# Four mLSTM projections as sixteen pairs of seven products each, made ahead of the attention, with the convolution summed in a PSUM bank

## The chip, the cores and the metric

One core of a Trainium2 chip. The metric is the device time of one execution of the whole program, in microseconds (us). The program works in fp32; matrix products run in the fp32r format, three of them for each product (below).

## The reference

A block on x (1024 positions, 1024 channels) with two branches and a gated sum. Cut to what matters:

```python
h = rmsnorm(x, norm_g)
proj = einsum('bsd,de->bse', h, w_in)      # a_q a_k a_v a_o a_z a_g b_q b_k b_v b_z g_a g_b, 1024 columns each, a_g 16
qk = silu(centred_depthwise_conv(concat([a_q, a_k]), ml_conv_w))    # width 5, along the sequence
mq, mk, mv = heads(qk[:1024]), heads(qk[1024:]) / 16, heads(a_v)    # 4 heads of 256
hm = rmsnorm(mlstm(forward) + mlstm(backward), ml_norm_g)           # gates from a_g
y_a = hm * sigmoid(a_o) * silu(a_z)
att = rmsnorm(diff_attention(rope(b_q), rope(b_k), b_v, lam), da_subln_g) * (1 - lambda_init)   # 8 heads
y_b = att * silu(b_z)
mix = sigmoid(g_a + gb0) * (y_a @ w_branch_a) + sigmoid(g_b + gb1) * (y_b @ w_branch_b)
return rmsnorm(x + mix @ w_out, final_g)
```

## The kernel before, in words

Every fp32 matrix is held as a high part (H, rounded to fp32r) and a low part (L, the rest), and a product of two is three fp32r products into one PSUM bank: wH x hH, wH x hL, wL x hH. A weight block of 128 columns (`load_w`) comes by DMA into `raw`; ScalarE copies it to `wH`, and GpSimd (POOL) or, in the mLSTM, VectorE subtracts to get `wL`. `proj` makes one block's product with half the sequence: 8 steps of k by three parts, 24 matmuls of 128x512 into one of the two banks `pj`. `v_units` makes v with 256 columns at a time, 192 matmuls of 128x256 a head.

The program is laid out by `build` as a list of units with costs and due times; `Weaver.weave` merges lists by when a unit is ready (table `LAG`) and by its share of its list. What comes out is each engine's order; nothing reorders it on the chip. The stages: x is loaded, normalised and transposed (TensorE, `transpose_x`), split into `hH`, `hL` (`split_h`); the attention's angles and rotary tables; eight attention heads; the mLSTM (pool `w2`), four heads, here numbered 0 to 3; the two branch products and the output.

`fill(n)` gives n units of the gates g_a and g_b, 48 matmuls each, which may stand anywhere; the table `FILL` says how many stand at each place.

In the mLSTM a head n goes through `ml_proj`: the projections of v, k and q, with the convolution on VectorE over the whole 1024 positions in SBUF (`cin` to `acc` or `hm`, L803), a split of the result into akH, akL, aqH, aqL (L808, L809), and a second list `oz`, the o and z projections, whose eight 24-matmul units are woven into the head's core. `ml_core` works in chunks of 256 positions, both directions. A state step transposes k (L130, into a bank T), weighs it into kwH and kwL (ScalarE L882, VectorE L883), multiplies it with v (L126) and adds it to the state C (L904, L906), which is split into CH and CL (L916, L917). Then come eight tiles of scores: SS = k x q, I = state x q (one bank each), weights W on VectorE (L947, L954), denominators (L961 to L970), W scaled and summed over directions (L974, L976), its transposes, their split WH and WL (L994, L995), PO = W x v, and hm, the sum of I and PO (L982, L1006). At the end of each head y_a is formed with the gates `gA`, made of `oz` (L824 to L831).

```python
            pr, oz = self.ml_proj(n, stm[n])
            core, tail, out = self.ml_core(n, stm[n])
            cut = len(pr) * 2 // 3
            w.weave(late, pr[:cut])
            w.add(*pr[cut:])
            w.weave(core, oz + fill(FILL[10 + n]))
            late = tail + out
```

## Time and profile before

| | |
|---|---|
| three runs | 1762.59 to 1762.73 us, median 1762.73 |
| the profiled execution | 1761.77 us, its span 1760.1 |
| TensorE clock granted, mean | 0.994 |
| TensorE busy | 1700.8 us |
| VectorE busy | 990.7 us |
| ScalarE busy | 709.7 us |
| GpSimd busy | 320.6 us |
| mean DMA rate | 90 GB/s |

The span is from the first to the last instruction of the profiled execution; 1.67 us of its time lie around it. Shares and busy times are means over stages with different limits, so the mLSTM, the opening and the attention are read by windows of their own.

### The profile page before, as it was taken

How to read it: one execution, taken by the hardware profiler on the slowest of the kernel's cores; microseconds unless marked ns; L12 is line 12 of the kernel's file. 1: busy time of each engine (PE TensorE's matmuls, PEld its weight loads, DVE VectorE, ACT ScalarE, POOL GpSimd, SP SyncE). 2: the span in 40 equal slices, each digit the busy share in tenths (PEclk: the TensorE clock that was granted, in tenths of full speed). 3: DMA queues.
4: the chain of work that ended last, by engine and by line, in shares of the span. 5: the costliest groups of instructions: out<-in, count | busy, mean ns of one | idle time of the engine just before them, and what ended most of it. 6: DMA issues, size and time to landing. Idle time of an engine off the chain costs nothing.

```text
span 1760.1 us, 23869 instructions
## 1 busy us (share of the span) xinstructions
PE 1700.8 (97%) x9311; PEld 1449.3 (82%) x9311; DVE 990.7 (56%) x1915; ACT 709.7 (40%) x1354; POOL 320.6 (18%) x300
## 2 busy tenths in 40 slices
PE   6999899999999999999999999999999999999998
PEld 5788788879878987887888888888888888888886
DVE  6326466666666665542577476656838743125533
ACT  5225455444445554441344344434434433122211
POOL 2323142331243233111000000100000002222000
PEclk9999999999999999999999999999999999999999
DMA  4445252345154515213210221121111117444222
GB/s 160 120 108 128 65 137 68 78 127 138 42 134 106 129 36 149 82 50 96 78 48 25 61 63 34 49 72 42 43 48 61 37 43 265 136 142 134 84 85 83
DMA packets 146787, 157.74 MB, mean 90 GB/s; under 512 B 7881, under 2 KB 106594, under 8 KB 146674
## 3 DMA queue, kind: packets, MB, share of 16 engines
q1 hardware_dynamic: 146498, 156.19, 31.5%
q8 instruction: 73, 1.20, 0.3%
q14 instruction: 40, 0.33, 0.1%
q10 hardware_dynamic: 176, 0.02, 0.0%
HBM read 118.31 MB, written 37.88 MB: 89 GB/s over the span
## 4 chain that ended last, share of the span: by engine, by line
PE 84%; DVE 4%; DMA 3%; POOL 3%; issue 3%; ACT 2%; SPq 0%; POOLq 0%; DVEq 0%; ACTq 0%
PE pj L242 50%; PE pj L264 9%; PE S L656 5%; PE PV L692 4%; PE pj L1149 4%; PE T L130 4%; PE T L126 2%; PE I L126 2%; PE SS L126 1%; PE PO L126 1%; DMA stk<-hl 1%; DMA rb<-rsd 1%; POOL m L599 1%; DMA qL<-stk 1%; ACT e L660 1%
## 5 line engine op out<-in xcount | busy, mean ns | idle before, releaser
L242 PE MATMUL pj<-hH,wH 128*128 128x512 f32 x1152 | 466.0, 404 | 7.6 <-ACT gt L568 4.6
L242 PE MATMUL pj<-hH,wL 128*128 128x512 f32 x1152 | 456.8, 397 | 0.6 <-POOL wL L185 0.6
L242 PE MATMUL pj<-hL,wH 128*128 128x512 f32 x1152 | 456.4, 396 | 0.0
L242 PEld LDWEIGHTS pj<-hH,wL 128*128 128x128 f32 x1152 | 217.3, 189 | 53.7 <-POOL wL L185 1.1
L242 PEld LDWEIGHTS pj<-hH,wH 128*128 128x128 f32 x1152 | 217.5, 189 | 52.9 <-ACT gt L568 5.0
L242 PEld LDWEIGHTS pj<-hL,wH 128*128 128x128 f32 x1152 | 217.5, 189 | 44.8
L660 ACT ACTIVATE e<-S,nm 128x1024 f32<-128x1024 f32 x128 | 143.0, 1117 | 186.6 <-DVE nm L658 186.4
L681 DVE TENSOR_TENSOR pL<-T,pH 128x512 fp32r<-128x512 f32 x128 | 87.9, 687 | 150.6 <-ACT pH L680 150.5
L658 DVE TENSOR_REDUCE nm<-S 128x1 f32<-128x1024 f32 x128 | 155.7, 1217 | 23.8 <-PE S L656 23.6
L200 POOL TENSOR_TENSOR wL<-raw,wH 128x1024 fp32r<-128x1024 f32 x45 | 109.1, 2425 | 308.6 <-ACT wH L195 301.5
L195 ACT CAST wH<-raw 128x1024 fp32r<-128x1024 f32 x88 | 92.3, 1049 | 172.6 <-PE pj L242 137.3
L264 PE MATMUL pj<-wH,hH 128*128 128x256 f32 x512 | 143.6, 281 | 0.0
L264 PE MATMUL pj<-wL,hH 128*128 128x256 f32 x512 | 143.2, 280 | 0.0
L264 PE MATMUL pj<-wH,hL 128*128 128x256 f32 x512 | 143.0, 279 | 0.0
L242 PE MATMUL pj<-sl_yb,wH 128*128 128x512 f32 x384 | 119.1, 390 | 0.3 <-DVE sl_yb L1065 0.2
L264 PEld LDWEIGHTS pj<-wH,hH 128*128 128x128 f32 x512 | 96.0, 187 | 1.1
L264 PEld LDWEIGHTS pj<-wH,hL 128*128 128x128 f32 x512 | 96.2, 188 | 0.8
L264 PEld LDWEIGHTS pj<-wL,hH 128*128 128x128 f32 x512 | 96.1, 188 | 0.0
L198 DVE TENSOR_TENSOR wL<-raw,wH 128x512 fp32r<-128x512 f32 x86 | 57.5, 691 | 64.9 <-ACT wH L195 64.4
L667 DVE SCALAR_TENSOR_TENSOR e<-e,r,e 128x1024 f32<-128x1024 f32 x64 | 92.7, 1448 | 1.2
L656 PE MATMUL S<-kst,qH 128*128 128x512 f32 x256 | 90.2, 432 | 2.7 <-DMA kst<-stk 2.7
L680 ACT CAST pH<-T 128x512 fp32r<-128x512 f32 x128 | 74.7, 583 | 32.5 <-PE T L130 29.5
(312 smaller groups left out, 3048.6 us busy)
## 6 DMA issues: line engine op xcount, KB each, us to landing
raw<-in_w_in_dram SPq DMA_DIRECT2D x88, 512.0 KB
stk<-hl SPq DMA_DIRECT2D x64, 256.0 KB
qH<-stk SPq DMA_DIRECT2D x32, 256.0 KB
qL<-stk SPq DMA_DIRECT2D x32, 256.0 KB
kst<-stk SPq DMA_DIRECT2D x16, 512.0 KB
x<-in_x_dram SPq DMA_DIRECT2D x8, 512.0 KB
tgb<-gt SPq DMA_DIRECT2D x16, 256.0 KB
rb<-rsd SPq DMA_DIRECT2D x16, 256.0 KB
```

The source lines that it names most:

```text
L126: self.t.matmul(out, lhsT=l, rhs=r, start=(i == 0), stop=(i == n - 1))
L130: self.t.transpose(out, in_, self.ident[0:k, 0:k])
L195: self.a.copy(wH, raw)
L200: self.p.tensor_tensor(out=wL, in0=raw, in1=wHf, op=ALU.subtract)
L242: self.t.matmul(ps, lhsT=l[:, k, :], rhs=r, start=(n == 0), stop=(n == 23))
L264: self.t.matmul(ps[:, i, :], lhsT=l, rhs=r[:, k, :], start=(kh == 0 and k == 0 and m == 0), stop=(kh == 1 and k == 3 and m == 2))
L656: self.t.matmul(ps[:, o], lhsT=x[:, j, c], rhs=st["k"][:, j, o], start=first, stop=not first)
L658: v.tensor_reduce(out=nm, in_=ps, axis=AX.X, op=ALU.max, negate=True)
L660: a.activation(out=e, in_=ps, func=AF.Exp, bias=nm[:, 0:1], accum_out=Z[:, j, t:t + 1])
L667: v.scalar_tensor_tensor(out=e0, in0=e, scalar=r[:, 0:1], in1=e0, op0=ALU.mult, op1=ALU.add)
L680: a.copy(pH[:, :, s], ps)
L681: v.tensor_tensor(out=pL[:, :, s], in0=ps, in1=pH[:, :, s].bitcast(F32), op=ALU.subtract)
```

## The change

The products of q, k, o and z leave the mLSTM. Two weight blocks of 128 columns, both halves of the sequence and both halves of the sum over channels make a product of 2x2 by 2x2 blocks, which is done with seven block products in place of eight (a scheme of Winograd's: sums of the blocks of w and of h first, then sums of the products). There are 16 such pairs: for each head two blocks of k, one o with one z, two blocks of q, the other o with the other z.

- Opening: besides hH and hL, four combinations of h's blocks are formed and split (`first_part`, `sums`: TH, TL, in a new pool `tf`). The blocks are transposed in the order 0, 4, 1, 5, 2, 6, 3, 7. Two more gate units stand there (four in place of two), and the low part of a weight block is subtracted on GpSimd in eight pieces.
- Pairs (`pair_units`): each of the seven products has 12 matmuls into one of six banks T; VectorE adds the products up from the banks (L283, L317, L342). `load_form` makes the seven forms of the weights: sums on GpSimd, the high part on ScalarE, the low part on VectorE for three forms and on GpSimd for four.
- Convolution (`conv_sink`): in a bank T, 512 positions at a time, ScalarE's first factor and four steps on VectorE, after each pair of k or q; the result goes to DRAM (`cd`). The product of the gates of o and z goes to DRAM as well (`gd_ml`). That is 24 arrays of 0.5 MB.
- mLSTM: `ml_proj` fetches the convolved k and q (`kf`, `qf`) and the gates by DMA from SyncE's queue and splits k and q; it has no `oz` units any more. v's units are woven with the end of the head before.
- Tables: FILL has one gate unit in place of two at the first place, two in place of three at two further ones, and one each in the cores of heads 0 to 2 (none in head 3, which alone had one); LAG's W goes from 22 to 2, out from 34 to 14, aq from 1.2 to 9. The rest after the mLSTM has three gate units where there were four.

```diff
-FILL = (2, 0, 0, 0, 0, 0, 0, 3, 3, 0, 0, 0, 0, 1)
+FILL = (1, 0, 0, 0, 0, 0, 0, 2, 2, 0, 0, 1, 1, 1, 0)
...
+    def load_form(self, key):
...
+        a.copy(H, src)
+        (self.v if f in (0, 4, 6) else g).tensor_tensor(out=Lo, in0=src, in1=H.bitcast(F32), op=ALU.subtract)
...
+    def pair_units(self, p, sink):
...
+        plan = lambda: (B(0, 0), T(1), T(2), T(0), B(0, 4), B(1, 4), T(3))
...
+            if k0 == 0:
+                box["ps"] = self.bank("T")
...
+            for k in range(k0, k0 + 2):
+                for m, (l, r) in enumerate(((wH, bH), (wH, bL), (wL, bH))):
+                    self.t.matmul(ps, lhsT=l[:, k, :], rhs=r[:, k, :], start=(k == 0 and m == 0), stop=(k == 3 and m == 2))
...
+            if f == 0:
+                box["p1"] = u("p1", 2)
+                a.copy(box["p1"], ps)
+            elif f == 1:
+                box["u2"] = u("u2")
+                add(box["u2"], box["p1"])
+            elif f == 2:
+                box["u3"] = u("u3")
+                add(box["u3"], box["u2"])
+            elif f == 3:
+                sink(1, 1, ps, box["u3"])
+                add(box["u2"], box["u2"])
+            elif f == 4:
+                sink(0, 0, ps, box["p1"])
+            elif f == 5:
+                sink(0, 1, ps, box["u2"])
+            elif f == 6:
+                sink(1, 0, ps, box["u3"])
...
+    def conv_sink(self, seg, n):
...
+            v.tensor_tensor(out=raw[:, 2 + j * 512:2 + (j + 1) * 512], in0=ps, in1=rest, op=ALU.add)
...
+            for half in range(2):
+                o = half * 512
+                acc = self.bank("T")
+                th = self.s0.tile([128, 512], F32, name="tz", tag="tz", bufs=2)
+                a.mul(acc, raw[:, o:o + 512], w(0))
+                for x in range(1, 5):
+                    v.scalar_tensor_tensor(out=acc, in0=raw[:, o + x:o + x + 512], scalar=w(x), in1=acc, op0=ALU.mult, op1=ALU.add)
+                a.activation(out=th, in_=acc, func=AF.Tanh, scale=0.5)
+                v.scalar_tensor_tensor(out=y[:, o:o + 512], in0=th, scalar=1.0, in1=acc, op0=ALU.add, op1=ALU.mult)
+            self.q.dma_start(out=self.cd[seg][2 * n + i], in_=y)
...
+    def sums(self, pool, k, half):
...
+        v.scalar_tensor_tensor(out=t2, in0=ps, scalar=g, in1=t1, op0=ALU.mult, op1=ALU.subtract)
+        p.tensor_tensor(out=f[:, 0], in0=t2, in1=f[:, 0], op=ALU.subtract)
+        p.tensor_tensor(out=f[:, 1], in0=f[:, 1], in1=t2, op=ALU.subtract)
+        t = (t1, t2, f[:, 0], f[:, 1])
+        for i in (1, 0, 2, 3):
+            self.a.copy(self.TH[i][:, k], t[i])
+            (v if i < 2 else p).tensor_tensor(out=self.TL[i][:, k], in0=t[i], in1=fb(self.TH[i][:, k]), op=ALU.subtract)
...
+            q.dma_start(out=f, in_=self.cd[seg][2 * n + i])
...
-            v.tensor_tensor(out=Lo[:, i, :], in0=acc, in1=H[:, i, :].bitcast(F32), op=ALU.subtract)
+            a.copy(H[:, i, :], f)
+            v.tensor_tensor(out=Lo[:, i, :], in0=f, in1=H[:, i, :].bitcast(F32), op=ALU.subtract)
...
+            for i in range(len(self.pairs)):
+                w.add(*self.pair_units(i, sinks[i]))
...
-                cut = len(pr) * 2 // 3
-                w.weave(late, pr[:cut])
-                w.add(*pr[cut:])
-                w.weave(core, oz + fill(FILL[10 + n]))
+                if n == 0:
+                    pr = pr + fill(FILL[10])
+                w.weave(late, pr)
+                w.weave(oz + core, fill(FILL[11 + n]))
```

**Where the instructions stand.** TensorE, head 1, from a state step to the first scores, before (kf's predecessor here is acc, pj are the o and z products; of a run of like rows one is shown):

```order
L130 MATMUL T_9867<-ident_100,acc_9448 128x128
...
L242 MATMUL pj_9861<-hH1_120,wH_9630 128x512
...
L242 MATMUL pj_9909<-hH0_119,wH_9707 128x512
...
L126 MATMUL T_9914<-vH_9218,kwH_9865 128x258
...
L126 MATMUL T_9922<-vH_9218,kwH_9865 128x258
...
L242 MATMUL pj_9909<-hH0_119,wH_9707 128x512
...
L130 MATMUL T_9941<-ident_100,acc_9448 128x128
...
L126 MATMUL SS_9964<-akH_9419,aqH_9591 128x256
...
L126 MATMUL I_9971<-CH1_9959,aqH_9591 128x258
...
L242 MATMUL pj_9909<-hH0_119,wH_9707 128x512
```

and now:

```order
L130 MATMUL T_11755<-ident_124,kf_11360 128x128
...
L126 MATMUL T_11767<-vH_11461,kwH_11753 128x258
...
L126 MATMUL T_11775<-vH_11461,kwH_11753 128x258
...
L130 MATMUL T_11785<-ident_124,kf_11360 128x128
...
L126 MATMUL T_11796<-vH_11461,kwH_11783 128x258
...
L126 MATMUL T_11804<-vH_11461,kwH_11783 128x258
...
L130 MATMUL T_11814<-ident_124,kf_11360 128x128
...
L126 MATMUL SS_11828<-akH_11358,aqH_11368 128x256
...
L126 MATMUL I_11835<-CH1_11823,aqH_11368 128x258
```

Between the transposes of k and the state products, and ahead of the scores, stood projection matmuls; now nothing stands between them.

VectorE at the end of head 1, before (tz and gA belong to the gates of o and z):

```order
L974 TENSOR_SCALAR W0_10532<-W0_10532,rr_10549 128x256
L976 SCALAR_TENSOR_TENSOR W0_10532<-W1_10537,rr_10549,W0_10532 128x128
...
L995 TENSOR_TENSOR WL_10582<-T_10578,WH_10581 128x256
L1006 TENSOR_TENSOR hm_9963<-PO_10592,hm_9963 128x256
...
L830 SCALAR_TENSOR_TENSOR tz_10588<-tz_10588,pj_10500 128x512
L995 TENSOR_TENSOR WL_10606<-T_10602,WH_10605 128x256
L831 SCALAR_TENSOR_TENSOR gA_10006<-gA_10006,tz_10588 128x512
L1006 TENSOR_TENSOR hm_9963<-PO_10609,hm_9963 128x256
```

and now (akL and aqL are those of head 2, kf and qf what was fetched from DRAM):

```order
L1124 TENSOR_SCALAR W1_12278<-W1_12278,rr_12290 128x256
L977 TENSOR_TENSOR akL_12378<-kf_12379,akH_12377 128x1024
L1126 SCALAR_TENSOR_TENSOR W1_12278<-W0_12273,rr_12290,W1_12278 128x128
L977 TENSOR_TENSOR akL_12378<-kf_12383,akH_12377 128x1024
L1111 TENSOR_TENSOR qn_12329<-I_12311,gc_sint_10615 128x1
...
L1156 TENSOR_TENSOR hm_11827<-PO_12343,hm_11827 128x256
L1114 TENSOR_SCALAR ab_12332<-den_12318 128x2
L1145 TENSOR_TENSOR WL_12357<-T_12353,WH_12356 128x256
L1115 TENSOR_TENSOR den_12318<-den_12318,ab_12332 128x2
L977 TENSOR_TENSOR aqL_12388<-qf_12389,aqH_12387 128x1024
...
L1156 TENSOR_TENSOR hm_11827<-PO_12360,hm_11827 128x256
```

Three splits of the next head's k and q, of 1024 columns each, stand among the last tiles' rows, ahead of the hm that follow; the two gate rows are gone.

VectorE in the opening, from the first transposed block of the second half, before:

```order
L352 SCALAR_TENSOR_TENSOR hL1_122<-T_404,g_in_160,hH1_120 128x512
L352 SCALAR_TENSOR_TENSOR hL1_122<-T_411,g_in_160,hH1_120 128x512
L352 SCALAR_TENSOR_TENSOR hL1_122<-T_418,g_in_160,hH1_120 128x512
...
L352 SCALAR_TENSOR_TENSOR hL1_122<-T_453,g_in_160,hH1_120 128x512
L377 COPY pos_464<-T_462 128x8
L380 TENSOR_TENSOR ang_466<-pos_464,inv_133 128x256
```

and now (wH_785 is the first form of the first pair, written by its low half):

```order
L538 SCALAR_TENSOR_TENSOR hL1_149<-T_468,g_in_195,hH1_147 128x512
L515 SCALAR_TENSOR_TENSOR t12_475<-T_468,g_in_195,f_316 128x512
L538 SCALAR_TENSOR_TENSOR hL1_149<-T_477,g_in_195,hH1_147 128x512
L518 SCALAR_TENSOR_TENSOR t12_475<-T_477,g_in_195,t12_475 128x512
L524 TENSOR_TENSOR TL0_154<-t12_475,TH0_150 128x512
L538 SCALAR_TENSOR_TENSOR hL1_149<-T_495,g_in_195,hH1_147 128x512
L524 TENSOR_TENSOR TL1_155<-t12_475,TH1_151 128x512
...
L524 TENSOR_TENSOR TL1_155<-t12_556,TH1_151 128x512
L563 COPY pos_649<-T_647 128x8
L566 TENSOR_TENSOR ang_651<-pos_649,inv_168 128x256
L259 TENSOR_TENSOR wH_785<-raw_777,wH_785 128x512
```

Rows for t12 and TL stand between the hL, and a row that waits for a pair's weights stands among the angles.

More of the change, by code (lines that the diff above doesn't have):

```diff
@@ L198, in load_w @@
                     self.v.tensor_tensor(out=wL[:, k], in0=raw[:, k], in1=wHf[:, k], op=ALU.subtract)
+            elif self.opening:
+                for k in range(8):
+                    self.p.tensor_tensor(out=wL[:, k], in0=raw[:, k], in1=wHf[:, k], op=ALU.subtract)
             else:
@@ L202, in load_w, with pair_raws @@
         self.wt[key] = (wH, wL)
+    def pair_raws(self, p):
+        if p >= len(self.pairs) or p in self.praws:
+            return
+        self.praws[p] = raws = []
+        for seg, i in self.pairs[p]:
+            pool = self.wpool if p % 2 == 0 else self.s0
+            t = pool.tile([128, 8, 128], F32, name="raw", tag="raw", **({} if p % 2 == 0 else dict(bufs=2)))
+            o = OFF[seg] + 128 * i
+            self.q.dma_start(out=t, in_=self.A["w_in"][0][:, o:o + 128].rearrange("(k p) e -> p k e", p=128))
+            raws.append(t)
@@ L217, in run @@
                 need = max(order.index(k) for k in u.keys) + 1
-                while nxt < len(order) and (nxt <= need or nxt == need + 1 and len(self.wt) < 3):
+                room = lambda k: sum(1 if x[0] == "sw" else 2 for x in self.wt) + (1 if k[0] == "sw" else 2) <= 6
+                while nxt < len(order) and (order[nxt][0] != "sw" or hasattr(self, "_s0")) and (nxt < need or nxt <= need + (4 if order[nxt][0] == "sw" else 1) and room(order[nxt])):
                     self.load_w(order[nxt])
@@ L1220, in begin @@
                 self.hL = [self.hpool.tile([128, 8, 512], F32R, name=f"hL{i}") for i in range(2)]
+                self.TH = [self.tf.tile([128, 4, 512], F32R, name=f"TH{i}") for i in range(4)]
+                self.TL = [self.tf.tile([128, 4, 512], F32R, name=f"TL{i}") for i in range(4)]
                 keys = [g[0].keys[0] for g in (g0, g1)]
@@ L1272, in build @@
             w.add(do(lambda: setattr(self, "ml", True)))
-            w.add(enter("w2", "w2"), banks("ps2", T=2, SS=1, PO=1, I=1))
+            w.add(enter("w2", "w2", side="right"), banks("ps2", T=2, SS=1, PO=1, I=1))
             w.banks.update(T=2)
@@ L1291, in build @@
             w.weave(loads, rest[cut:])
[L1293 removed]
+            w.add(leave("h"), enter("wr", "wr"))
             passB = self.mix_units("gb", st3)
```

201 lines of the change are left out of this document (137 added, 64 removed).

## The prediction

> **What bounds the kernel now.** I read the page's busy times first, then the chain of work that ended last, then windows of the mLSTM, whose filler the change takes away.
>
> ```profile
> PE 1700.8 (97%) x9311; PEld 1449.3 (82%) x9311; DVE 990.7 (56%) x1915; ACT 709.7 (40%) x1354; POOL 320.6 (18%) x300
> PE 84%; DVE 4%; DMA 3%; POOL 3%; issue 3%; ACT 2%; SPq 0%; POOLq 0%; DVEq 0%; ACTq 0%
> ```
>
> TensorE is busy in 97% of the span, so only 59.3 us (1760.1 - 1700.8) are idle: whoever removes matmuls wins their time only if no idle time takes their place. The chain in head 1's mLSTM shows how that idle time is kept away:
>
> ```profile
> 1053.39 5.60 PE pj L242 x24
> 1058.99 1.44 PE T L126 x12
> 1060.43 2.09 PE pj L242 x9
> 1062.52 0.44 PE T L130 x4
> 1062.96 5.60 PE pj L242 x24
> 1068.56 1.44 PE T L126 x12
> ...
> 1131.19 22.62 PE pj L264 x192
> ```
>
> Between the transposes of k (L130) and the state products (L126) stand 24 projection matmuls (L242): 5.60/24 = 0.2333 us each, the price of a 512-wide matmul here. They are the o and z projections, and they cover the time that ScalarE and VectorE need. (The last row is v's projection of the next head, 0.118 each.) By windows of the whole mLSTM, then of head 1's state steps, its eight tiles, and in the tiles its fillers (pj), late weight parts (wL) and gates (tz):
>
> ```profile
> core 0: us, PE busy (x) PEld busy (x) DVE busy (x) ACT busy (x) POOL busy (x), PEclk, DMA share, GB/s
> 860.00:930.00 70.00, 69.33 (x326) 56.49 (x325) 45.44 (x61) 30.08 (x42) 1.89 (x10) 1.00 0.17 47
> 930.00:981.00 51.00, 48.53 (x316) 43.55 (x314) 42.66 (x167) 25.19 (x63) 4.67 (x17) 1.00 0.15 42
> 981.00:1131.20 150.20, 147.65 (x871) 128.92 (x870) 97.27 (x237) 62.67 (x118) 7.29 (x28) 1.00 0.17 50
> 1131.20:1280.70 149.50, 146.94 (x866) 128.35 (x866) 96.58 (x236) 62.68 (x118) 7.20 (x27) 1.00 0.17 50
> 1280.70:1420.00 139.30, 137.99 (x802) 120.24 (x801) 83.86 (x184) 55.04 (x97) 5.05 (x16) 1.00 0.16 46
> 1052.80:1084.00 31.20, 31.20 (x161) 26.20 (x160) 20.07 (x31) 12.44 (x20) 0.13 (x2) 1.00 0.18 51
> 1084.00:1131.20 47.20, 44.65 (x298) 40.46 (x297) 40.18 (x161) 23.73 (x60) 4.78 (x18) 1.00 0.12 34
> ```
> ```profile
> 1084.00:1131.20 47.20, 20.32 (x78) 13.50 (x78) 1.37 (x2) 2.37 (x4) 1.00 0.12 34
> ```
> ```profile
> 1084.00:1131.20 47.20, 10.05 (x26) 4.73 (x26) 2.15 (x3) 0.00 (x0) 1.00 0.12 34
> ```
> ```profile
> 1084.00:1131.20 47.20, 2.70 (x4) 1.18 (x2) 1.00 0.12 34
> ```
>
> From 860 to 1420 TensorE idles 0.67 + 2.47 + 2.55 + 2.56 + 1.31 = 9.6 us over four heads. In the tiles 78 of 298 matmuls are fillers: 78 x 0.2333 = 18.2 us, so the core's own TensorE work is 44.65 - 18.2 = 26.5 us. VectorE is busy 40.18 us there, of which 2.15 (wL) and 2.70 (tz) go with the fillers: 35.3 us remain. Without fillers VectorE, not TensorE, bounds the tiles.
>
> **The change, part by part.**
>
> *Fewer products.* Each of 16 pairs takes 7 x 12 = 84 matmuls where 8 x 12 = 96 stood (1536 to 1344 in all): 192 x 0.2333 = -44.8 us. They were TensorE-bound before, so all of it counts. The remaining 1344 x 0.2333 = 313.6 us are moved ahead of the attention.
>
> *The cores without filler.* The order shows no projection matmul left between the state steps or the tiles; heads 0 to 2 keep one gate unit of 48 matmuls, ahead of the first state products, head 3 none. What then lies bare in a state step is this:
>
> ```profile
> 1071.94 0.60 PE L130 MATMUL T<-ident,acc 128*128 128x128 f32 x4
> ...
> 1072.57 0.59 ACT L879 COPY kn<-T 128x512 f32<-128x512 f32 x1 [0.54 <-PE T L130]
> ...
> 1074.60 0.48 DVE L883 SCALAR_TENSOR_TENSOR kwL<-T,gc_ws,kwH 128x256 fp32r<-128x256 f32 x1 [0.54 <-ACT kwH L882]
> ```
>
> From the transposes' end (1072.54) to the last weighted part (1075.08) are 2.54 us, with the step to TensorE some 2.7. Of a head's three steps the gate unit covers one: 5.4, and about 1.1 for converting the new state, 6.5 us; 9.2 in head 3, 4 in head 0, whose first steps have gate work beside them. In a tile the chain runs from I through the denominators to hm:
>
> ```profile
> 1095.29 0.16 DVE L961 TENSOR_TENSOR qn<-I,gc_sint 128x2 f32<-128x2 f32 x1 [0.69 <-PE I L126]
> 1097.96 0.48 DVE L982 SCALAR_TENSOR_TENSOR hm<-I,al,hm 128x256 f32<-128x256 f32 x1
> ```
> ```profile
> PE I L126 <- DVE hm L982: 5.2, 4, 1.3
> PE pj L242 <- ACT wH L184: 3.1, 1, 3.1
> ```
>
> Even with fillers the next tile's I (one bank) waited for hm four times, 5.2 us. Bare, the tiles cannot be under VectorE's 35.3. If every tile is one serial chain they take 26.5 of TensorE plus 8 x 3.35 (from 1095.29 to 1098.44, and 0.2 to reach VectorE), 53 us. I take 39, VectorE's 35.3 plus eight waits of about 0.5 (0.69 in the row): nearer to the lower end since other tiles' operations fill the queue meanwhile. Idle: 39 - 26.5 = 12.5 per head.
>
> *The tail of a head.* The next head's akL and aqL now stand in VectorE's queue between the last tiles' operations, and wait for ScalarE's copies and the DMAs that fetch the convolved q and k from DRAM. Everything behind them, hm included, waits too.
>
> ```profile
> L809 DVE TENSOR_TENSOR akL<-acc,akH x8: 1215/1219/1226, 881.0 to 1338.9; 128x1024 fp32r<-128x1024 f32 x8
> ```
>
> Three such ahead of the last hm, 3.66 us, and about one wait of 1: 4.6 for heads 0 to 2 (0 if they fall into VectorE's gaps).
>
> *Head 0's start.* The gates' chain is long:
>
> ```profile
> 830.60 0.74 DVE L451 TENSOR_SCALAR gts<-pj,bias 16x512 f32<-16x512 f32 x1 [2.12 <-PE pj L445]
> ...
> 849.20 0.32 DVE L498 COPY gb<-hm 32x1 f32<-32x1 f32 x2
> ...
> 863.37 0.23 DVE L553 COPY dec<-T 128x64 f32<-128x64 f32 x1 [0.23 <-PE T L130]
> ```
>
> From gts to gb are 18.6 us, and in the changed order 156 of v's matmuls stand beside them, 18.4 us: even, but four akL and aqL (4.9 us) with their fetches now lie in VectorE's queue among the chain, +6. From gb to dec are another 14 us, stretched by filler; I reckon 10 bare, and only v's last 36 matmuls (4.2 us) are left, where the q and k projections stood: +6. Together +12 (3 to 20).
>
> Together: 4 + 12.5 + 4.6 + 12 = 33 in head 0, 6.5 + 12.5 + 4.6 = 23.6 in heads 1 and 2, 9.2 + 12.5 = 21.7 in head 3; 102 less the 9.6 that was there, **+92**. The low end, with tiles at 35.3, 4.4 for a head's state waits, no tail and no gate chain, is 4 x (8.8 + 4.4) - 9.6 = +43; the high end, serial tiles (14 more per head), +148.
>
> *Opening.* VectorE makes, for each transposed block of h, hL and now also t12 and TL:
>
> ```profile
> 38.43 5.36 DVE L352 SCALAR_TENSOR_TENSOR hL<-T,g_in,hH 128x512 fp32r<-128x512 f32 x8 [2.19 <-ACT hH L351]
> ```
>
> Eight hL took 5.36; with 8 t12 and 8 TL at the same 0.67 it is 16 us. So the eighth block comes near 54 and not 43.8, the second gate unit waits for it, and the angles and the tables behind it in the queue move too. POOL adds 16 subtractions:
>
> ```profile
> L185 POOL TENSOR_TENSOR wL<-raw,wH x32: 1262/1287/1564, 32.8 to 612.0; 128x512 fp32r<-128x512 f32 x32
> ```
>
> 16 x 1.29 = 20.6 us, 42 to 63. Two more gate units (2 x 48 x 0.2333 = 22.4 us, taken from places further on) stand against it. I take +9, the wait of the first gate unit's second half for the eighth block:
>
> ```profile
> 40.71 0.50 PE L242 MATMUL pj<-hH,wH 128*128 128x512 f32 x1
> ```
> ```profile
> 54.31 0.75 DVE L419 TENSOR_SCALAR cosT<-T,scol 128x512 f32<-128x512 f32 x1 [0.21 <-PE T L130]
> ```
>
> It began at 40.71 and reaches the eighth block 21 matmuls later, at 45.6, against 54; the tables (54.31) come near 70, and the gate units cover them or not: ends 0 and 16.
>
> *The pair stage.* Two pairs (one with convolution) take 168 x 0.2333 = 39.2 us of TensorE. VectorE does 14 drains, 20 convolution steps, 6 subtractions of weights and 4 gate steps, 44 operations of 512 columns:
>
> ```profile
> L830 DVE SCALAR_TENSOR_TENSOR tz<-tz,pj x16: 679/686/690, 922.6 to 1422.8; 128x512 f32<-128x512 f32 x16
> ```
>
> 44 x 0.686 = 30.2 us: hidden on the average, not in bursts. Convolution sums and products share six banks; the third product of the next pair needs a bank that a sum frees about 9.4 us after the product that completed its input, while TensorE arrives after 8.4. So +1 on 8 pairs, less where TensorE comes later: +7 (0 to 25). POOL's 8 x 1.29 = 10.3 us in 19.6 are hidden; were they not, each form would stop a product for up to 1.3. The 24 arrays of 0.5 MB that go to DRAM and back find queues at a share of 0.17.
>
> *Attention with three gate units fewer* (one at the first, two at later places): +3, since its own chains are covered by projections; ends 0 and 11.
>
> The sum: 1760.1 - 44.8 + 92 + 9 + 7 + 3 = 1826 of span, and 1.7 around it (the profiled execution is 1761.77): **1828 us**. That execution stands 0.96 below the median of 1762.73, which I do not add.
>
> **The clock.** A bare TensorE can also lose its clock. Once in this trace it did:
>
> ```profile
> 114.00:115.00 1.00, 0.00 (x0) 1.00 1.03 309
> 118.00:119.00 1.00, 1.00 (x3) 0.50 0.00 0
> ```
>
> After the 3.1 us wait for wH above, the granted clock was 0.50 for some 7 us; three matmuls filled a microsecond that takes over four otherwise. One such drop costs 7 x 0.5 = 3.5 us. The bare waits of 2.7 that I expect are just shorter than that one. [...]
>
> **The rivals.**
> - *The bare chains are shorter.* The tiles run at VectorE's floor, the tail and the gate chain fall into gaps: heads +43 to +60, opening and pairs 0 to 8: 1775 to 1805. For it: VectorE's queue is in another order now, with more of the next tile's work between; against it, the 5.2 us of waits for hm even with filler.
> - *The clock drops in the bare stretches.* One drop in each head is 4 x 3.5 = +14, 1842; three in each +42, 1870. For it, the 3.1 us wait; against it, 2.7 is below it.
> - *The pairs don't pay*, since VectorE or a bank stops TensorE at nearly every pair: 25 instead of 7, 1846. It decides when VectorE's two pairs, with their waits, go over 39.2 against 30.2 counted.
> - *The other side, not slower.* The cores bare cost no more than the 44.8 saved. With opening 4 and the rest at nothing, the heads may cost 40.8, with state steps at 4.4 tiles under 26.5 + (40.8 + 9.6)/4 - 4.4 = 34.7 us. That is the point of decision, 0.6 below VectorE's own 35.3; it needs that VectorE's operations run shorter without the stream of filler beside them. 1750 to 1764.
>
> **How the numbers follow.** My forecast, bare cores as summed (1806 to 1842): 0.54. Shorter chains 0.16, clock 0.13, pairs that don't pay 0.08, the other side 0.09. The measurement tells about 0.2% (3.5 us) from no change. Faster by more than that has 0.06 (most of the other side), within it 0.03, slower 0.91. The range leaves out the other side and the upper part of the clock's: 1775 to 1862.
>
> **What would show it.** In the changed trace: TensorE's busy time near 1656 (1700.8 - 44.8); windows of a head's eight tiles near 39 us with VectorE over 35 and TensorE at 26.5; waits of TensorE for kwL near 2.7 us, for I on hm and for WL in the tail; a first wait of several us near 45 for hL; a granted clock of 1.00 in the cores. Heads' windows with under 10 us of idle each would prove the sum wrong, as would waits of more than 1 us in every pair, or a clock below 0.9 in the mLSTM's slices.

## The result, and the profile after

The changed kernel takes 1863.28 us (median of four runs, 1856.09 to 1868.83) against 1762.66 of before: a ratio of 1.0572, 95% interval 1.0533 to 1.0611. The forecast was 1828 with a range of 1775 to 1862; the direction and the place were right, the amount lies just outside, on the slow side. The profiled execution of after is the fastest of the four (1856.09, span 1854.3).

The page of after, first the busy times, then the granted clock in 40 slices:

```profile
PE 1703.6 (92%) x9119; PEld 1444.3 (78%) x9119; DVE 1086.1 (59%) x2103; ACT 750.0 (40%) x1474; POOL 518.9 (28%) x470
...
PEclk8899999999999999999999999989999989999999
```

TensorE has 192 matmuls fewer and is busy 2.8 us longer; the forecast had it busy for some 1656 us, and it was 1703.6. That was the first sign that its matmuls ran slower, and the granted clock shows it: eights in the opening and in the mLSTM, where before all slices were nines. By stages (opening, pairs, attention, heads 0 to 3, the part after the mLSTM, the output; the columns are those of the windows in the prediction):

```profile
0.00:95.10 95.10, 61.32 (x276) 49.76 (x277) 51.88 (x116) 47.65 (x78) 55.67 (x75) 0.89 0.35 110
95.10:405.20 310.10, 310.10 (x1344) 251.75 (x1343) 243.16 (x340) 130.44 (x224) 168.76 (x151) 1.00 0.31 93
405.20:1143.80 738.60, 707.59 (x4073) 611.07 (x4073) 437.71 (x634) 337.47 (x696) 223.11 (x146) 0.99 0.39 99
1143.80:1256.80 113.00, 88.48 (x558) 76.70 (x557) 73.41 (x248) 47.80 (x99) 6.30 (x21) 0.91 0.33 105
1256.80:1352.40 95.60, 78.51 (x529) 70.83 (x529) 55.67 (x193) 38.95 (x90) 6.90 (x20) 0.95 0.24 78
1352.40:1448.00 95.60, 78.54 (x530) 70.88 (x530) 55.65 (x193) 38.86 (x90) 6.91 (x20) 0.95 0.24 78
1448.00:1545.40 97.40, 81.57 (x524) 73.47 (x523) 52.24 (x191) 35.58 (x90) 7.25 (x15) 0.89 0.10 33
1545.40:1665.00 119.60, 115.58 (x490) 92.27 (x490) 29.60 (x32) 28.43 (x31) 23.93 (x10) 0.97 0.52 167
1665.00:1854.30 189.30, 181.91 (x806) 147.60 (x804) 86.77 (x158) 44.81 (x83) 20.09 (x14) 0.99 0.32 106
```

The same windows of before, the opening, the attention and the whole of the mLSTM's first head:

```profile
0.00:55.60 55.60, 38.02 (x180) 31.74 (x181) 38.64 (x97) 30.41 (x49) 17.25 (x21) 1.00 0.47 151
55.60:823.00 767.40, 743.64 (x4217) 637.31 (x4217) 432.39 (x634) 343.59 (x704) 228.19 (x153) 0.99 0.39 99
823.00:981.70 158.70, 155.07 (x895) 131.52 (x894) 109.98 (x285) 67.63 (x123) 6.68 (x28) 1.00 0.21 59
```

Stage by stage, with the work that moved taken out (a 24-matmul product at 5.6 us, a gate unit at 11.2):

| stage | forecast | measured | how |
|---|---|---|---|
| fewer products | -44.8 | -44.8 | 192 x 0.2333; the pair stage runs at 310.1/1344 = 0.2307 a matmul |
| opening | +9 | +17.1 | 95.1 - 55.6 - 22.4 for two more gate units |
| pair stage | +7 | -3.5 | 310.1 - 313.6, not one idle microsecond |
| attention | +3 | +4.8 | 738.6 - 767.4 + 33.6 for three gate units fewer |
| mLSTM to the end | +92 | +120.6 | 710.5 - 937.1 + 358.4 moved out - 11.2 for one gate unit more |
| sum of span | +66 | +94.2 | 1854.3 - 1760.1 |

Head 1 alone, in three parts: v and the tail of head 0, the gate unit with the state steps, the tiles:

```profile
1256.80:1283.20 26.40, 26.40 (x209) 26.40 (x209) 6.87 (x14) 7.81 (x16) 1.77 (x3) 0.93 0.18 61
1283.20:1304.90 21.70, 19.31 (x103) 15.47 (x102) 9.94 (x20) 6.97 (x13) 0.00 (x0) 1.00 0.47 146
1304.90:1352.40 47.50, 32.80 (x223) 28.96 (x222) 38.86 (x161) 24.18 (x62) 5.13 (x17) 0.93 0.17 56
```

The tiles take 47.5 us where the sum had 39, and 4.6 for the tail. VectorE is busy 38.9 of them, 35.3 and the three splits of the next head's k and q. The longest waits of TensorE in the whole trace:

```profile
PE I L126 <- DVE hm L1132: 21.6, 16, 2.1
PE I L126 <- ACT hm L1130: 12.1, 8, 2.5
...
PE PO L126 <- ACT WH L1144: 11.4, 19, 0.8
PE T L130 <- ACT f L507: 10.4, 1, 10.4
PE pj L402 <- DVE hL L538: 9.1, 2, 4.8
...
PE T L126 <- ACT kwH L1032: 7.4, 7, 1.1
PE T L130 <- DVE W L1124: 5.7, 3, 1.9
...
PE T L130 <- DVE hm L721: 4.0, 1, 4.0
```

The next tile's I waits for hm 24 times, 33.7 us, where before it did so 4 times, 5.2 us. None of the waits in the mLSTM's cores reaches 2.6 us (the 4.0, L721, stands in the gates' chain ahead of head 0's core), and yet the clock falls. One of these waits stands in head 1's last tiles (windows of 0.4 us, TensorE alone: busy time, granted clock):

```profile
1336.40:1336.80 0.40, 0.40 (x4) 1.00 0.00 0
1336.80:1337.20 0.40, 0.01 (x1) 1.00 0.00 0
...
1338.40:1338.80 0.40, 0.00 (x0) 1.00 0.00 0
1338.80:1339.20 0.40, 0.32 (x2) 1.00 0.00 0
1339.20:1339.60 0.40, 0.40 (x4) 0.51 0.00 0
```

After 2.1 idle microseconds the clock is 0.50 from 1339.2 to 1342.6, 3.41 us. Until the last instruction the trace has 19 stretches at half clock, each 3.41 us long or two or three times that, 102 us together with TensorE busy in 82 of them; before had 4 stretches, 17 us, busy 16.4. From the first gate product on, after has 13 stretches, 68 us, TensorE busy in 59: by estimate half of that, 29.5 us, is time that these matmuls would not have taken at full clock.

In after's trace all these stretches begin on one grid of 3.41 us, each within 0.01 us of it. Here are five neighbouring steps of the grid, the first just ahead of the drop above:

```profile
1335.80:1339.21 3.41, 1.33 (x12) 1.00 0.01 2
1339.21:1342.62 3.41, 2.75 (x14) 0.50 0.60 193
1342.62:1346.04 3.42, 1.63 (x13) 1.00 0.39 114
1346.04:1349.45 3.41, 1.28 (x9) 1.00 0.00 0
1349.45:1352.86 3.41, 2.68 (x11) 0.50 0.48 159
```

A step with TensorE busy for 1.33 us (39%) is followed by half clock, one with 1.63 us (48%) is not, one with 1.28 us is again. From the first gate product on, 11 of the 13 drops follow a step at 19 to 44%, while 12 steps at 47 to 65% kept the clock. The other two drops, at 1206 and 1482, follow steps at 65% that hold a bare state step.

### The profile page after: what moved, and what is told of

It reads as the page before. It is cut to its first block, busy times and chain, and to the rows that moved or that the text cites. A ratio compares the mean times of both kernels' runs of the same rounds, so it can differ in the third digit from the quotient of the medians.

```text
span 1854.3 us, 24316 instructions
## 1 busy us (share of the span) xinstructions
PE 1703.6 (92%) x9119; PEld 1444.3 (78%) x9119; DVE 1086.1 (59%) x2103; ACT 750.0 (40%) x1474; POOL 518.9 (28%) x470
## 5 line engine op out<-in xcount | busy, mean ns | idle before, releaser
L402 PE MATMUL pj<-hL,wH 128*128 128x512 f32 x640 | 254.3, 397 | 9.1 <-DVE hL L538 9.1
L402 PE MATMUL pj<-hH,wH 128*128 128x512 f32 x640 | 259.5, 406 | 3.1 <-ACT wH L186 3.1
L402 PE MATMUL pj<-hH,wL 128*128 128x512 f32 x640 | 254.8, 398 | 0.4 <-POOL wL L187 0.4
L205 POOL TENSOR_TENSOR wL<-raw,wH 128x1024 fp32r<-128x1024 f32 x39 | 95.6, 2452 | 286.5 <-ACT wH L197 286.5
L402 PEld LDWEIGHTS pj<-hL,wH 128*128 128x128 f32 x640 | 122.9, 192 | 34.0 <-DVE hL L538 10.2
L402 PEld LDWEIGHTS pj<-hH,wH 128*128 128x128 f32 x640 | 123.1, 192 | 27.2 <-ACT wH L186 3.5
L402 PEld LDWEIGHTS pj<-hH,wL 128*128 128x128 f32 x640 | 122.5, 191 | 27.8 <-POOL wL L187 1.1
L1102 POOL TENSOR_SCALAR_AFFINE_SELECT W<-W 128x128 f32<-128x128 f32 x64 | 20.1, 314 | 361.5 <-DVE W L1126 185.2
L197 ACT CAST wH<-raw 128x1024 fp32r<-128x1024 f32 x56 | 58.7, 1049 | 148.4 <-PE pj L402 109.3
L356 DVE SCALAR_TENSOR_TENSOR T<-cin,cols,T 128x512 f32<-128x512 f32 x128 | 89.5, 752 | 8.2 <-ACT T L354 7.1
```

Source lines behind the costliest of these rows:

```text
L197: self.a.copy(wH, raw)
L205: self.p.tensor_tensor(out=wL, in0=raw, in1=wHf, op=ALU.subtract)
L356: v.scalar_tensor_tensor(out=acc, in0=raw[:, o + x:o + x + 512], scalar=w(x), in1=acc, op0=ALU.mult, op1=ALU.add)
L402: self.t.matmul(ps, lhsT=l[:, k, :], rhs=r, start=(n == 0), stop=(n == 23))
L1102: p.affine_select(out=dg, in_=dg, pattern=[[-sg, 128]], compare_op=ALU.is_ge, fill=0.0, base=0, channel_multiplier=sg)
```

## The experiments

The time between the first gate product and the first output product (1143.8 to 1757.6 in after, 613.8 us) is the mLSTM with what follows it; "half clock" below is the time at a granted clock of 0.5 from the first gate product to the last instructions, and how much of it TensorE was busy. These two columns are of the one profiled execution of each run; after's is the fastest of its four.

| run | median us | ratio to before | mLSTM part | half clock, busy |
|---|---|---|---|---|
| after | 1863.28 | 1.0572 (1.0533 to 1.0611) | 613.8 | 68, 59 |
| spread fillers | 1844.90 | 1.0464 (1.0436 to 1.0493) | 600.1 | 65, 56 |
| 45 us of dummies | 1853.41 | 1.0520 (1.0496 to 1.0545) | 609.7 | 44, 41 |
| 62 us of dummies | 1846.06 | 1.0480 (1.0465 to 1.0496) | 599.8 | 10, 9 |
| 100 us of dummies | 1864.67 | 1.0603 (1.0573 to 1.0632) | 620.4 | 7, 6 |
| splits on GpSimd | 1864.07 | 1.0584 (1.0568 to 1.0601) | 619.2 | 86, 64 |
| late splits | 1846.76 | 1.0499 (1.0471 to 1.0528) | 605.3 | 72, 62 |
| opening's order | 1860.04 | 1.0559 (1.0528 to 1.0590) | 615.3 | 75, 64 |
| three of these | 1836.42 | 1.0417 (1.0399 to 1.0435) | 592.7 | 48, 43 |
| eight products a pair | 1903.17 | 1.0803 (1.0775 to 1.0831) | 619.0 | 92, 76 |

**The fillers spread through the cores.**

```diff
-                w.weave(oz + core, fill(FILL[11 + n]))
+                w.weave(oz + core)          # in its order, then:
+                w.out += spread(done, fill(FILL[11 + n]))    # 3 matmuls of the gate unit after each step or two
```

> The changed kernel with the one gate unit (48 matmuls, 11.2 us) of heads 0 to 2 not ahead of the first state products but spread evenly through the head's core, 3 matmuls at a time; the work is the same. Theory A (the loss is the bare cores: 68 us more idle time there than before and 53 us of half clock that the idle time brings on): a filler between two waits hides up to its own length, so in three heads some 8 us of idle time each go and about half of the half-clock time: 1810 to 1840 against 1863. Theory B (the loss is the new work at other places: the split of fetched q and k in the tails, the opening): unchanged, 1855 to 1870.

1844.9, just past the forecast's slow end, and not wholly for its reason: it had about half of the half clock go, and that hardly changed (65 us of 68). TensorE is as busy as in after, so the gain is shorter waiting. The same matmuls, 34 us of them in three heads, are worth 18 us only because of where they stand. Waits for hm fall from 33.7 to 20.5 us:

```profile
PE I L126 <- DVE hm L1132: 12.7, 10, 2.1
...
PE I L126 <- ACT hm L1130: 7.8, 8, 1.5
```

**Is it the clock or the waiting?** Matmuls that nobody reads, ahead of the waits:

```diff
+            self.warm(4)        # 4 matmuls of 128x512 into an idle bank pj, between a tile's scores and its I
             inter = self.bank("I", (128, 2, 512))
...
+            self.warm(2)        # after the transposes of W, ahead of PO
```

> The changed kernel with matmuls that nobody reads ahead of the waits in the mLSTM's tiles: 4 of 128x512 (0.93 us) after each tile's scores, 2 (0.47 us) after each transpose of W; 45 us of TensorE's time in all, most of it in what was idle. If half clock costs what I reckon (TensorE busy 53 us longer in the mLSTM), the granted clock there goes to 0.97 or more and the time to 1820 to 1845. If half clock only stretches work that had time to spare, the time stays at 1855 to 1870 or rises by up to 20 where a dummy stands in the way.

1853.4, between the two forecasts: 10 us won, where 18 was the least that I expected. The mean clock of the whole trace rose no further than 0.974, since dummies stood in the tiles alone, and drops stayed at the state steps, the tails and the gates' chain (44 us of half clock where after had 68). So I put more of them:

> As the run with dummy matmuls, and more of them: 5 before each tile's I (9 in the last two tiles), 3 before each PO, 8 before the last two transposes of W, 4 before the state products of the opening steps, and 9, 6 and 16 in the gates' chain. Theory of the clock (TensorE works 60 us of the mLSTM at half clock, which costs 31): the granted clock between the first gate product and the last head goes to 0.98 or more, and the time falls by 20 to 30 below the changed kernel, to 1833 to 1845, since the dummies stand where TensorE waited. Rival (the half clock is hidden by the waits, or the dummies get in the way as much as they help): 1853 or more.

The clock came as forecast, one drop left after the first gate product, and the time did not: 1864.7, the rival's number. In the trace TensorE has hardly a wait left (16.5 idle us between its matmuls from the first gate product on, 78.8 in after), and 100 us of dummies stand there. So the dummies were too many; that they delay the chains behind them is my reading of it. This run alone can't tell the theories apart, so the next has a size between:

> As the run with many dummy matmuls, which kept the clock up but took 100 us themselves where TensorE had some 88 us to spare: now 3 before each tile's I (6 in the last two), 2 before each PO, 6 before the last transposes, 4 before the second and third state products, 6, 5 and 14 in the gates' chain, 73 us in all. Theory of the clock: half-clock time in the mLSTM falls from some 60 us of TensorE's work to under 15, which saves 20, and little of the dummies stands in the way: 1838 to 1850, against 1853 with 45 us and 1865 with 100 us of dummies. Rival (a us of half clock costs nothing, what the dummies win they win by chance): 1853 to 1866.

1846.1, inside the range. It holds 265 dummies, which at 0.2333 are 62 us and not the 73 that I had counted. The same stretch of time in this run and then in after, from the first gate product on; this run is further along at its end (columns: length, busy time and count of TensorE, its loads, VectorE, ScalarE and GpSimd, then the clock):

```profile
1143.80:1590.00 446.20, 419.49 (x2629) 357.50 (x2628) 256.44 (x844) 184.52 (x388) 37.77 (x79) 0.99 0.30 98
```
```profile
1143.80:1590.00 446.20, 367.68 (x2303) 323.69 (x2302) 252.56 (x840) 178.73 (x385) 34.50 (x77) 0.92 0.28 92
```

With 62 us of matmuls added, the part is 14.0 us shorter. I see no way but the clock by which work that nobody needs can shorten a kernel: half-clock work fell by 50 us, worth 25 at full clock by the estimate above, and about 11 of it the dummies took back. After's own four runs point the same way without an edit: mean clocks of 0.972, 0.964, 0.962 and 0.958 go with 1856.1, 1865.3, 1861.2 and 1868.8 us (the two in the middle stand the other way round, and four runs can't tell cause from effect).

**The tail.** The splits of the next head's k and q, moved to GpSimd:

```diff
-            v.tensor_tensor(out=Lo[:, i, :], in0=f, in1=H[:, i, :].bitcast(F32), op=ALU.subtract)
+            p.tensor_tensor(out=Lo[:, i, :], in0=f, in1=H[:, i, :].bitcast(F32), op=ALU.subtract)
```

> The changed kernel with the low parts of the fetched k and q (akL, aqL) subtracted on GpSimd, which is busy 7 of 95 us a head, not on VectorE. In the changed kernel's trace three of them, 3.7 us, run on VectorE among the last tiles of heads 0 to 2, ahead of rows that the next I and the last transposes wait for. Theory of the tail: 3 to 4.5 us less in each of three heads and about one half-clock window less in one or two of them: 1845 to 1855 against 1863. Rival (VectorE has the time, the tiles wait for their own chain): 1858 to 1868.

1864.1: the rival's number, but not for its reason. In after they stand where the forecast had them. VectorE's rows in head 1's tail, and the transposes that wait for the last of them:

```profile
1343.07 1.23 DVE L977 TENSOR_TENSOR akL<-kf,akH 128x1024 fp32r<-128x1024 f32 x1
1344.21 0.35 DVE L1126 SCALAR_TENSOR_TENSOR W<-W,rr,W 128x128 f32<-128x128 f32 x1
1344.47 1.22 DVE L977 TENSOR_TENSOR akL<-kf,akH 128x1024 fp32r<-128x1024 f32 x1
...
1347.30 1.21 DVE L977 TENSOR_TENSOR aqL<-qf,aqH 128x1024 fp32r<-128x1024 f32 x1
```
```profile
1349.72 0.77 PE L130 MATMUL T<-ident,W 128*128 128x128 f32 x2 [1.89 <-DVE W L1124]
```

On GpSimd each takes 2.4 us, and the mask of the last tile's W queues behind three of them; TensorE then waits 3.3 us once a head:

```profile
1350.75 4.74 POOL L977 TENSOR_TENSOR akL<-kf,akH 128x1024 fp32r<-128x1024 f32 x2 [1.29 <-ACT akH L976]
1355.45 2.33 POOL L977 TENSOR_TENSOR aqL<-qf,aqH 128x1024 fp32r<-128x1024 f32 x1
1357.74 0.29 POOL L1102 TENSOR_SCALAR_AFFINE_SELECT W<-W 128x128 f32<-128x128 f32 x1
```
```profile
1358.74 0.77 PE L126 MATMUL PO<-vH,WH 128*128 128x256 f32 x2 [3.33 <-DVE den L1116]
```

The cost had moved to another queue. So the splits were made late instead, by a true dependence:

```diff
-            a.copy(H[:, i, :], f)
+            # one = 0 * ssq[:, 7:8] + 1, from the head before: exists only after its last tile
+            a.mul(H[:, i, :], f, st["one"][:, 0:1])
```

> The changed kernel with the split of the fetched k and q of heads 1 to 3 made to wait for the last tile of the head before (its high part is multiplied by a one that is made from that tile's sum of squares), so that akL and aqL leave the tail on every engine and run beside v's projection. On GpSimd they had stood in the tail too, ahead of a mask of W (three waits of 3.3 us). Theory of the tail: 3 to 4.5 us less in each of three heads, with the clock 1846 to 1856 against 1863. Rival (the tail waits for its own chain all the same): 1859 to 1867.

1846.8, at the fast end of the tail theory. The edit has a second part: the splits also stand behind the first four of v's units in TensorE's list. In the profiled execution the half clock is what it was (72 us, 68 in after), so there the gain is waiting alone, and the mLSTM part is 8.5 us shorter. The medians differ by 16.5; the rest goes with a higher clock of the runs not profiled (0.964 to 0.970, 0.958 to 0.964 in after) and with their spread (1846.3 to 1857.6 here), and is not explained further.

**The opening.**

```diff
-            w.add(do(lambda: ([self.norm_x(self.p0, i) for i in range(4, 8)], self.params())))
+            w.add(do(lambda: [self.norm_x(self.p0, i) for i in range(4, 8)]))
...
-            w.add(*g0[:k], *g1[:k], *tx)
-            w.add(*g0[k:], *g1[k:], do(lambda: (self.angles(self.p0), self.lam(self.p0))), *g2)
+            w.add(*g0[:4], do(self.params), *g0[4:k], *g1[:k], *tx, *g2[:k])
+            w.add(*g0[k:], *g1[k:], do(lambda: (self.angles(self.p0), self.lam(self.p0))), *g2[k:])
```

> The changed kernel with two changes in the opening's order on TensorE: the transpose of the parameter rows stands after the first 12 matmuls of the first gate unit, not ahead of it, and the first half of the third gate unit (24 matmuls, 5.6 us) ahead of the halves that wait for hL. If the opening's 17 us are the waits for hL (9.0), the rows behind first_part (3.7 later start) and the half clock after them (3), 8 to 14 of them go: 1849 to 1855. Rival (VectorE's own row of work sets when the tables come, and the wait moves there): 1858 to 1866.

1860.0, the rival; the 3 us less than after lie within both intervals. The opening's waits in this run, where after had 9.1 for hL and 1.9 for the tables' rep:

```profile
PE T L130 <- DVE rep L593: 7.9, 1, 7.9
PE pj L402 <- ACT f L507: 4.6, 1, 4.6
PE pj L402 <- DVE hL L538: 4.5, 1, 4.5
```

VectorE's row of work sets when the tables come; TensorE, covered earlier, waits there. The opening ends 2.7 us earlier (first pair product at 92.2 against 94.9).

**Three together:** the spread fillers, the late splits and this order.

> The spread gate units (1845), the late split and the opening's other order (1860) in one kernel. If they are separate losses: 1845 less 7 to 14 for the split, less 3 for the opening, 1826 to 1836. If the spread fillers already hid the tail: 1838 to 1845.

1836.4, on the border of the two forecasts and 27 below after; alone the three won 18, 16.5 and 3 by the medians, together 38, so they overlap by some 11. Here the half clock falls too, to 48 us. What the bare cores cost is not repaired by placing 34 us of filler well: 74 us against before are left.

**Are seven products worth it?** Each pair as eight:

```diff
...
-        return [Unit(6 * MM, lambda f=f, k0=k0: product(f, k0), (("sw", p, f),)) for f in range(7) for k0 in (0, 2)]
+        un = []
+        for j in range(2):
+            for i, (seg, c) in enumerate(self.pairs[p]):
+                un += self.proj(("w_in", OFF[seg] + 128 * c), j, lambda ps, i=i, j=j: sink(i, j, ps, None))
```

> The changed kernel with each pair made as eight products of 24 + 24 matmuls in place of seven (one block and half at a time, no sums of weights, the drain a plain copy); place, convolution in the bank, DRAM and mLSTM are as in the changed kernel, and the sums of h are still formed. If the pair stage is bound by TensorE, as its 310 us for 1344 matmuls say, it takes 192 matmuls longer: +44, 1900 to 1915. If VectorE or the banks bound it (the rival), less than half of that: 1863 to 1885.

1903.2, 40 more than after, as forecast: the saving is real at nearly its full size, and the pair stage is TensorE's (in the profiled execution the first gate product comes 46.3 us later than in after). Moving the products ahead without saving any costs some 141 us against before (0.0803 of 1762); the seven products give 40 of them back.

**Giving the cores their cover back.** o and z return to the cores, q and k stay as eight pairs:

```diff
-                    self.pairs.append((("ao", 2 * n + i), ("az", 2 * n + i)))
-                    sinks.append(self.oz_sink(2 * n + i))
...
-                w.weave(oz + core, fill(FILL[11 + n]))
+                w.weave(core, oz + fill(FILL[11 + n]))     # oz: the 24-matmul projections of before
```

> Only q and k as pairs ahead of the attention (8 pairs); o and z are again eight 24-matmul projections a head, woven into the core as in the kernel before. Theory A: the cores are covered, so idle time and clock in the mLSTM are near those of before (under 4 us idle a head, clock 0.99); 8 pairs save 8 x 12 x 0.2333 = 22.4 us and the opening and the attention lose 17 and 5 as measured in the changed kernel: 1755 to 1775. Theory B: the tails and fetches still cost, 1790 or more.

1797.9 (ratio 1.0212, 1.0183 to 1.0240): 65 us better than after, but 23 worse than the forecast for it, and the number of the rival (1790 or more). The half clock from the first gate product on falls to 20 us: one drop in head 0, one at its end, and none from there to the part after the mLSTM. Part of the miss is a new wait: pairs with convolution now stand back to back, where o and z stood between them:

```profile
PE T L280 <- DVE y L358: 9.3, 6, 1.7
```

The bank wait that the forecast put at +7 in the changed kernel exists, but only where no other pair stands between. Three repairs together:

```diff
-        (self.v if f in (0, 4, 6) else g).tensor_tensor(out=Lo, in0=src, ...)
+        g.tensor_tensor(out=Lo, in0=src, ...)      # with the splits on GpSimd and the opening's order
```

> The version with o and z back in the cores (1798) with three more edits: the low parts of k and q on GpSimd, the opening in the order of the other run, and all low parts of the weight forms on GpSimd, not three of seven on VectorE. In that version the pairs with convolution stand back to back and take 168.6 us for 672 matmuls where 155 would do, as VectorE has some 21 us for 19.6 of TensorE. If these three are its losses beside the fillers: 10 from the opening, 8 to 12 from the pairs, 3 to 8 from the tails, 1765 to 1780. If the pairs wait for banks and not for VectorE's sum, or the mLSTM's loss is its own chain: 1785 or more.

1803.1, a miss: the pairs ran at 155.0 us for 672 matmuls as expected, but in the heads it was all lost again, where GpSimd runs three splits ahead of a mask of W (1116.8 to 1123.8 at the end of head 0) and TensorE then stops for up to 4.6 us:

```profile
PE PO L126 <- ACT WH L1158: 17.0, 7, 4.6
```

With the late splits on VectorE in their place, which changes both their engine and their time:

> The version with o and z back in the cores (1798) with the weight forms' low parts on GpSimd, the opening's other order and the late split, but k and q split on VectorE: on GpSimd they had stopped TensorE for over 3 us at the start of each head. The pairs win 12 (155.0 us against 168.6 in the trace), the opening 3, the tails 3 to 9: 1774 to 1784. If what the mLSTM loses there (25 us against the kernel before) is the split's fault, down to 1765; if the pairs' gain is given back behind them, 1790 or more.

1775.6 (1.0082, 1.0067 to 1.0097), as forecast. The first matmuls of v in heads 1 and 2 of this run:

```profile
1117.04 0.27 PE L424 MATMUL pj<-wH,hH 128*128 128x256 f32 x1
```
```profile
1233.02 0.28 PE L424 MATMUL pj<-wH,hH 128*128 128x256 f32 x1
```

A head takes 116.0 us; before's 149.5 less 8 products of 5.6 and with one gate unit of 11.2 more is 115.9. That shows the main point from the other side: with cover, nothing is lost in these heads by fetching q and k from DRAM, by the late splits or by the pairs.

Two more runs looked for the 14 us that this version still lacks against its sum (1762 - 22.4 for eight pairs + 17.1 and 4.8 for opening and attention as in after, 1761.5). Gate units taken from the cores and given to the ends:

```diff
-FILL = (1, 0, 0, 0, 0, 0, 0, 2, 2, 0, 0, 1, 1, 1, 0)
+FILL = (1, 0, 0, 0, 0, 0, 0, 2, 3, 0, 0, 0, 0, 0, 1)
```

> The best version so far (1776: eight q and k pairs ahead, o and z in the cores, late split, weight forms' low parts on GpSimd) with the gate units where the cores no longer need them taken back: none in heads 0 to 2, one in head 3, four after the mLSTM, seven in the attention. In its trace a head takes 116.0 us, which is what 149.5 less 44.8 plus a gate unit of 11.2 gives, but the part from head 3's v to the end is 14 us longer than it should be, with 7 us of half clock at 1501 and waits for the loads of y. If that part lacks cover: 8 to 14 less, 1762 to 1768. If cover there is worth nothing (the rival: the half clock and the waits stay as in the kernel before), 1772 to 1778.

1778.8 (1.0098, 1.0084 to 1.0112): the rival, and no gain; the heads lose what the ends win (drops of the clock come back at the ends of heads 1 and 2, 3.41 us each, from 1229.5 and 1338.5). And half of a gate unit ahead of the tables:

```diff
-            w.add(..., *g2[k:])
+            w.add(..., *g2[k:], *g3[:k])       # and only g3[k:] ahead of the pairs
```

> The same and the first half of the fourth gate unit (24 matmuls, 5.6 us) ahead of the transposes of the rotary tables, which TensorE waits 7.8 us for. If the wait simply shrinks: 5 to 8 less than the run without it, with the half clock that it brings on. If the first pair's forms then lack their cover (the rival), within 2 us of it.

1772.3 (1.0064, 1.0049 to 1.0078), 6.5 less, as forecast. None of the versions beats the kernel before. What the last one still loses is some 8 in the opening, 8 in the attention and 20 from the first gate product on, against 24 won in the pairs; which waits make the 20 stays open.

## Why the prediction was right or wrong

- **Fewer products, -44.8:** right. The pair stage ran without an idle microsecond, and taking the seven products away cost 40.
- **The cores without filler, +92 of waiting:** right in size. TensorE's idle time in the heads and after them is 85.9 us (24.5 + 17.1 + 17.1 + 15.8 + 4.0 + 7.4, span less TensorE's busy time by stage) against 18 before, 68 more. TensorE is also busy 52.7 us longer there than the work explains (624.6 against 919.1 - 358.4 + 11.2); the half clock takes 29.5 of that, and the other 23 I put down to the edges of short bursts. From the first gate product on, after's TensorE idles 93 times between its matmuls, before's in the same part 13 times; behind such a wait the first 128x258 matmul stands with 0.39 us (at 1315.07), the last of the burst with 0.28, where those between start 0.12 apart. By estimate that is 0.27 a burst, 22 us for 80 more of them. No run measures them alone; counted as waiting they make 91 together. Its parts were off both ways: a bare state step takes 4.2 us for 1.9 of work, 2.3 bare and not 2.7; a bare set of tiles 47.5, and not 39 and 4.6, with some 3 of it from half clock.
- **The tail, 4.6 a head:** right in kind. Three splits at 1.22 stand in it; making them late won 8.5 us of three heads in the profile, 2.8 a head, and 16 by the medians.
- **The clock, priced at nothing: this step failed.** The sum of span fell short by 28 us (the median lies 7 above the profiled execution, with a lower clock), and this is its largest part. The forecast said that bare waits of 2.7 us are "just shorter" than the one after which the clock had dropped in before's trace, 3.1 us, kept the sum at full clock and made the drops a rival. But before's trace has four drops, the other three after waits of 4.57, 3.41 and 2.53 us, and the last of these is under 2.7. In after no single wait in the cores reached 2.6 us, and the clock dropped all the same: 13 times after the first gate product, for 68 us, and only two of the 13 follow a longer wait (the 4.0 of the gates' chain and one of 2.9 after the last head). That is some 29.5 us by estimate, as much as the 28.6 by which the mLSTM's term was too small. What went with the drops was not one long wait but how little TensorE was busy in the step of 3.41 us before: 19 to 44% ahead of 11 of the 13. The second rival, which I gave a chance of 0.13, fits what the trace shows. Before's wait of 2.53 us, and the clock behind it:

```profile
686.28 0.43 PE L692 MATMUL PV<-pL,vH 128*128 128x256 f32 x1 [2.53 <-DVE pL L681]
```
```profile
686.00:686.50 0.50, 0.22 (x1) 0.99 0.92 197
686.50:687.00 0.50, 0.50 (x4) 0.50 0.93 197
```

- **Opening, +9:** the wait was right (9.1 for hL), the term was not, +17.1. Missed were the transposes of the parameter rows, which now wait for `first_part` to empty a bank (10.4 us, so that the first gate product comes 4.0 later than before), and a stretch of half clock from 52 to 63 after the wait:

```profile
52.22 0.68 PE L402 MATMUL pj<-hL,wH 128*128 128x512 f32 x1 [4.79 <-DVE hL L538]
```

- **Pair stage, +7:** wrong, nothing; the wait shows only where pairs with convolution follow each other. **Attention, +3:** 4.8.
- **The other side** needed tiles under 34.7 us; they took 47.5.

The range's upper end, 1862, left out the upper part of the clock's rival, three drops a head at 1870; there were about three, cheaper ones (29.5 us for 13, not 42 for 12). That the direction came out right owes nothing to this step.

## What to carry to other kernels

Independent matmuls between the steps of a chain are not only work, they are the chain's cover; before moving them away for a saving, count the chain's idle time without them, and take the work's saving less that. Count the clock with it: in these traces 163 of the 165 steps of 3.41 us at full clock in which TensorE was busy for under 45% were followed by half clock, and in such a place of this kernel the next step's work has to be priced at half clock. A step that delayed VectorE's queue, moved to GpSimd, delayed that queue instead (TensorE then waited 3.3 us once a head); a dependence that makes it late took most of it off the chain here (2.8 of 4.6 us a head in the profile).

## What the runs showed of the hardware

- In these traces the granted clock fell to 0.50 for 3.41 us, or a multiple of it, each time on the trace's grid of 3.41 us, and in after's cores with no wait of 2.6 us. Over all 16 traces, without their first 80 us and their last 15, every one of the 131 steps at full clock with TensorE busy under 40% was followed by half clock, 32 of the 34 at 40 to 45%, 6 of the 26 at 45 to 50%, and 4 of the 139 at 50 to 65%. Of the steps at 65 to 70%, 19 of 90 were; in after the two such drops follow a bare state step (1.9 us of work in each 4.2), while the same steps in heads 1 and 2 kept the clock. Why they differ stays open. In runs where 62 and 100 us of dummies filled the gaps the mLSTM kept a clock of 0.99 and more.
- Before's four runs beside after's lie within 0.14%, after's four within 0.7%, its fastest with the highest mean clock (0.972) and its slowest with the lowest (0.958). The clock alone does not give the scatter: the runs with 45 us of dummies, 44 us of half clock in the profiled one, lie within 0.25%, those with 100 us of dummies, 7 us of half clock, within 0.53%.
- The subtraction of 128x1024 (L977) took 1.22 us on VectorE and 2.4 on GpSimd, so GpSimd, idle as it was, was no free place for a step on which a chain's mask waits.
